# Splitting the state updates off the sample group's DeltaNet stream

## The chip, the cores and the metric

The program runs on one core of a Trainium2 chip. A core has five engines with an instruction queue each: PE (TensorE, matrix products into the accumulators of PSUM), DVE (VectorE), ACT (ScalarE), POOL (GpSimd) and SP, which here only issues DMA transfers. A queue is served in order. The metric is device time in microseconds (us); lower is better.

## The reference, cut to what matters

One decoder layer is run for a prompt of 512 tokens and for a sample group of 8 sequences with 4 new tokens each; both share the weights, so the kernel carries their 544 columns together. The layer is a half-step SwiGLU, then a token mixer, then another half-step SwiGLU, each between RMS norms:

```python
proj = h @ p['w_in']                               # one projection, D_IN = 7696
o_dn, S_new = gated_delta_rule(q, k, v, g, beta, S0)    # branch A; S0 (8 seq, 8 heads, 128, 128)
o_dn = rmsnorm(o_dn, dn_norm) * silu(z)
o_sw = attend(q_sw, k_sw, v_sw, sinks)             # branch B, window 128
y = sigmoid(gate_a) * o_dn + sigmoid(gate_b) * o_sw
x = x + g2 * rmsnorm(y @ w_out, mix_norm_post)
```

For the sample group the delta rule starts from a stored state S0 per sequence and head. It gives two results: the outputs o (from q, the old state and the four new tokens), which go on into y, and the new state S = exp(g) S0 + k^T v, which goes only to the output `delta_sample`. The two share the corrected values v, and neither needs the other after that.

## The kernel before, in words

Activations lie transposed (channels on partitions, 544 tokens along the free axis, as two halves of 272). Every weight product is made from three products of split operands (`mm3`, L301: hi by xh, hi by xl, lo by xh). A unit of weights is a 256 KB load (`raw`, L279, 4 buffers), a cast on ACT (L270, `hi`) and a subtraction on DVE or POOL (L271, `lo`); two units make one output block of 128 channels (`pb`).

The order of the work is made by `Streams`: a main generator (the weight products) and side generators each yield `(cost, latency)`. `now` grows by the cost, and a side generator is due again at `now + 1.5 * latency`; all that are due are stepped before main goes on. Of several that are due, the one with the lower rank goes first. One unit of cost stands for about a microsecond of PE: 24 matmuls of `mm3` cost 2.8 units. The framework takes the order in which instructions were emitted as their priority and builds each engine's queue from that with a cost model of its own, so that an instruction emitted late can stand earlier in its engine's queue than ones emitted before it, if its inputs are there.

In the mixer main projects, in this order, heads (U0 to U3), keys, values, queries and the gates G0 to G7. Gate block b gives `gbs` (L1521), then `z` (L1528, L1534) and the sample's part of it, `zs` (L1535). Beside it run `delta_stream` (the prompt's DeltaNet, two heads at a time, whose last norm makes `ro0` and `prb`, L340 to L345 and L353), `merge_stream` (the prompt's merge into `osw`, L1555 and L1557) and `att_main`: the attention and, after it, `delta_sample(hg)` for head groups 0 and 1, one after the other, from one set of buffers (`sdn`, one copy of each tile, four of S0).

`delta_sample` goes through these steps: decays and products of keys (to L1624), the products with the old states (`pks`, L1638), the corrected values `svn` (L1647), the outputs and `stq`, the sum under the norm (L1659). Then it updates the states: `vm` on DVE (L1662), four scalings of S0 on POOL (L1667), eight products `psu` on PE (L1673), eight additions on DVE (L1677), four stores of 512 KB from SP (L1680). Only then comes the norm of the outputs: `pro` (L1682), `srx` (L1684), eleven small DVE instructions of `rsqrt` (`sroy`, `sroa`, L340 to L345), `prb` (L353), `so` (L1689), and the merge into `osw` (L1700, L1703, L1704), which needs `zs` of the group's four heads. `merged[8]` and `merged[9]` say that the two groups are merged.

After the gates main makes `y @ w_out`. The first two output blocks (b = 0, 1) take one unit of each first: rows 0 to 511, blocks 0 to 3 of `osw` (split into `hh` and `hl` by L270 and L271); this needs `merged[8]`. Then it waits for `merged[9]`, splits blocks 4 to 7, and emits the rest only when every side stream has ended:

```python
for b in range(4, 8):
    while not (mx.merged[b] and mx.merged[9]):
        yield 0.5
    L.split(hh[:, b, :], hl[:, b, :], mx.osw[:, b, :])
while sch.side:
    yield 0.5
mx.c_sp.close()
mx.ctx.close()
```

With that the mixer's pools are closed and new ones opened in their room. In these lie `xT` (2.2 MB, reloaded, L1940) and the twelve units of `w_out` for blocks 2 to 7, which are kept (`fhw`, `flw`) since the two halves of tokens are done one after the other. The first cast into `fhw` waits until all uses of the closed pools have ended, the stores from S0 among them. Each unit of such a block is 12 matmuls.

Of the kernel before, what the change touches and what calls it, by code (L numbers as in the profile page):

```python
# [10 lines left out]
F32 = mybir.dt.float32  # L11
# [3 lines left out]
ALU = mybir.AluOpType  # L15
# [4 lines left out]
P = 128  # L20
# [14 lines left out]
EPS = 1e-6  # L35
# [24 lines left out]
L_SMP = 0.8  # L60
# [727 lines left out]
class Mixer:  # L788
# [770 lines left out]
    def delta_sample(self, hg, sp):  # L1559

        nc, L, a = self.nc, self.L, self.a
        st = L.st
        hs = slice(4 * hg, 4 * hg + 4)
        col = slice(32 + hg, 33 + hg)
        k4 = self.kqs[:, hs, 0, :]
# [6 lines left out]
        E4 = grow.rearrange("p (h s t) -> p h s t", h=4, s=SB)  # L1572
# [13 lines left out]
        kdec = sp.tile([P, P], F32, tag="skdec", name="skdec")  # L1586
# [31 lines left out]
        tq = sp.tile([P, P], F32, tag="stq", name="stq")  # L1618
        nc.scalar.activation(out=tq, in_=qcf, func=AF.Square, scale=math.sqrt(EPS * 128.0))
        S0 = []  # L1620
# [6 lines left out]
        for i, src in enumerate((kc, qc)):  # L1627
            km = sp.tile([P, 4, SB, NS], F32, tag="km", name="km")
            nc.gpsimd.memset(km, 0.0)
            for h in range(4):  # L1630
# [3 lines left out]
                                        op=ALU.mult)  # L1634
            yield 0.0, 3.0 * L_SMP
            for s in range(SB):
                for h in range(4):
                    nc.tensor.matmul(out=pk[32 * h:32 * h + 32, i * P:(i + 1) * P], lhsT=km[:, h, s, :],  # L1638
                                     rhs=S0[h][:, s, :], start=s == 0, stop=s == SB - 1, skip_group_check=True)
# [6 lines left out]
        vn = sp.tile([P, P], F32, tag="svn", name="svn")  # L1646
# [8 lines left out]
        o = sp.tile([P, P], F32, tag="so4", name="so4")  # L1655
# [2 lines left out]
        nc.scalar.activation(out=o2, in_=oT, func=AF.Square, scale=128.0 ** -0.5)  # L1658
        nc.vector.tensor_tensor(out=tq, in0=tq, in1=o2, op=ALU.add)  # L1659
        yield 0.5, 0.6 * L_SMP  # L1660
        vm = sp.tile([P, SB, P], F32, tag="km", name="vm")
        nc.vector.tensor_tensor(out=vm, in0=vn.unsqueeze(1).to_broadcast([P, SB, P]),  # L1662
                                in1=L.c("SEQM").unsqueeze(2).to_broadcast([P, SB, P]), op=ALU.mult)
        for h0 in (0, 2):
            hs = (h0, h0 + 1)
            for h in hs:
                nc.gpsimd.tensor_tensor(out=S0[h], in0=S0[h], in1=E4[:, h, :, ST - 1:ST].to_broadcast([P, SB, P]),  # L1667
                                        op=ALU.mult)
            yield 0.0, 3.0 * L_SMP
            for s0 in (0, 4):  # L1670
                p3s = [L.wk("psu4") for _ in hs]
                for h, p3 in zip(hs, p3s):
                    nc.tensor.matmul(out=p3, lhsT=kdec[32 * h:32 * h + 32, :], rhs=vm[32 * h:32 * h + 32, s0:s0 + 4, :],  # L1673
                                     start=True, stop=True)
# [3 lines left out]
                yield 1.0, 0.5 * L_SMP  # L1678
            for h in hs:
                nc.sync.dma_start(out=a["delta_sample"][0, :, 4 * hg + h].rearrange("s k v -> k s v"), in_=S0[h])  # L1680
        pr = L.wk("pro4")
        nc.tensor.matmul(out=pr[:, :64], lhsT=tq, rhs=L.ones[:, :64], start=True, stop=True)  # L1682
        rx = st.tile([P, 1], F32, tag="srx", name="srx")
        nc.vector.tensor_scalar(out=rx, in0=pr[:, 0:1], scalar1=128.0 * EPS * EPS, scalar2=None, op0=ALU.add)  # L1684
        ro = L.rsqrt(rx, [P, 1], "sro")
        yield 0.3, 3.5 * L_SMP
        pb = L.wk("prb4")
        L.bcast_cols(ro, [(0, 0, P)], [pb[:, :P]], "sro")
        nc.vector.tensor_tensor(out=o, in0=o, in1=pb[:, :P], op=ALU.mult)  # L1689
        yield 0.3, 0.3 * L_SMP  # L1690
        while any(self.z[h] is None or not self.gb_done[h] for h in range(4 * hg, 4 * hg + 4)):
            yield 0.0, 1.0 * L_SMP
        self.merge_sample(hg, o)
        self.merged[8 + hg] = True

    def merge_sample(self, hg, o):
        nc, L = self.nc, self.L
# [68 lines left out]
    def plan(self, feed):  # L1766

        L, win, x = self.L, self.win, self.x
        self.att_done = [0] * 4
        self.kqv, self.z, self.gb_done = {}, [None] * NH, [False] * NH  # L1770
        self.od_done, self.merged = [False] * NH, [False] * 10
        self.decays_done = False
        self.odd = L.dr.tile([NH, P, SEQ], F32, name="odd")
        qT, kT = (lambda: self.qT), (lambda: self.kT)
        q = lambda c: [u for b in range(8) for u in L.project(win, Q0 + b * P, x, self.evac(qT, b, (c,)), cs=(c,),
                                                              pool_lo=False)]
        self.mark0 = feed.add(q(0))
        self.marks = []

        def ba(ps):  # L1780
            self.sch.spawn(self.decays(ps, self.rp), 0)

        for n in ORDER:
            if n == "B":
                us = L.project(win, BA0, x, ba, ncol=16)
            elif n == "Q":
                us = q(1)
            elif n == "K":
                us = [u for b in range(2) for u in L.project(win, K0 + b * P, x, self.evac(kT, b))]
            elif n == "V":  # L1790
                us = [u for b in range(2) for u in L.project(win, V0 + b * P, x, self.v_block(b))]
            elif n[0] == "U":
                us = self.head_blocks(int(n[1]))
            else:
                us = self.gate_blocks(int(n[1]))
            self.marks.append((n, feed.add(us)))
# [186 lines left out]
```

## Time and profile before

| | us |
|---|---|
| three runs, median (lowest, highest) | 1589.41 (1588.27, 1590.55) |
| the profiled execution, its own time | 1595.09 |
| its span in the trace | 1593.3 |

| engine | busy us | share of the span |
|---|---|---|
| PE | 1519.0 | 95% |
| DVE | 851.2 | 53% |
| ACT | 633.5 | 40% |
| POOL | 284.3 | 18% |

The busy share is an average over stages. PE is busy nearly throughout, so the stretches in which it isn't, and those in which its granted clock is below 1.00, are what can be given back without taking work away. A time in the trace counts from the start of the span. In a timeline, "x4" is a run of four instructions of one kind merged into a piece, and the bracket gives the idle time before it and what ended that. The matrix instructions of f32 operands (`psu`, `pks`, `pro`, `prb`) show as two matmuls each.

### The profile page before, as it was taken

The page shows a single profiled execution, that of the slowest core. Times are in us where ns is not written, and L with a number is a line of the kernel's source. Part 1 is how long each engine was busy: PE and PEld are TensorE (multiplying, and loading weights), DVE is VectorE, ACT ScalarE, POOL GpSimd, SP SyncE. Part 2 cuts the span into 40 slices and gives each one's busy share as a digit, 9 for nine tenths or more (in the row PEclk, how much of TensorE's full clock was granted, in tenths as well). Part 3 has the DMA queues.
Part 4 walks back from the last instruction along what each step waited for, and adds up shares of the span by engine and source line. Part 5 has one row for each costly group of instructions (what it writes and reads, how often), then busy time and mean ns, then how long its engine had stood idle before and what let it go on. Part 6 is the DMA issues. An engine that isn't in the chain of part 4 may idle for free.

```text
span 1593.3 us, 32457 instructions
## 1 busy us (share of the span) xinstructions
PE 1519.0 (95%) x12819; PEld 1410.3 (89%) x12819; DVE 851.2 (53%) x2080; ACT 633.5 (40%) x1397; POOL 284.3 (18%) x386
## 2 busy tenths in 40 slices
PE   7999999999998999998999999998979999999996
PEld 3699999999987999897788899897979999999995
DVE  5433322333588787468879757748374332233365
ACT  4322222322444554344676433233455332223363
POOL 1000000000353232123012012312548000000042
PEclk9999999999999999899999999998989999999999
DMA  9464444455556434554212325534425433333253
GB/s 316 152 197 134 142 151 146 151 159 152 180 157 188 118 90 101 137 146 96 57 37 73 91 71 140 154 84 137 132 65 159 109 86 88 92 88 92 80 149 117
DMA packets 314533, 199.64 MB, mean 125 GB/s; under 512 B 36464, under 2 KB 297331, under 8 KB 314092
## 3 DMA queue, kind: packets, MB, share of 16 engines
q1 hardware_dynamic: 314086, 197.46, 43.6%
q8 instruction: 100, 1.64, 0.4%
q14 instruction: 53, 0.43, 0.1%
q10 hardware_dynamic: 294, 0.11, 0.0%
HBM read 182.08 MB, written 16.36 MB: 125 GB/s over the span
## 4 chain that ended last, share of the span: by engine, by line
PE 79%; DVE 12%; ACT 4%; DMA 3%; issue 2%; POOL 1%; SPq 0%; DVEq 0%; ACTq 0%; POOLq 0%
PE pb L301 17%; PE pg L301 16%; PE pu L301 16%; PE pd L301 15%; PE adaps L467 3%; DVE y L1195 2%; DVE lo L271 1%; PE psc L1010 1%; ACT hi L270 1%; PE pov L1066 1%; PE pgu L301 1%; DVE xT L571 1%; PE pvn L1332 1%; PE ppt L1052 1%; ACT s L1031 1%
## 5 line engine op out<-in xcount | busy, mean ns | idle before, releaser
L270 ACT CAST hi<-raw 128x512 fp32r<-128x512 f32 (+2 forms) x502 | 287.8, 581 | 600.5 <-PE pu L301 172.7
L271 DVE TENSOR_TENSOR lo<-raw,hi 128x512 fp32r<-128x512 f32 (+2 forms) x368 | 252.9, 688 | 397.6 <-ACT hi L270 387.4
L301 PE MATMUL pb<-hh,hi 128*128 128x272 f32 (+1 forms) x1008 | 235.7, 304 | 4.6 <-ACT hh L270 1.8
L301 PE MATMUL pb<-hl,hi 128*128 128x272 f32 (+1 forms) x1008 | 227.6, 295 | 0.0
L301 PE MATMUL pb<-hh,lo 128*128 128x272 f32 (+1 forms) x1008 | 225.9, 295 | 0.3 <-DVE lo L271 0.2
L271 POOL TENSOR_TENSOR lo<-raw,hi 128x512 fp32r<-128x512 f32 (+1 forms) x104 | 136.4, 1316 | 478.5 <-ACT hi L270 461.0
L301 PEld LDWEIGHTS pb<-hh,hi 128*128 128x128 f32 (+1 forms) x1008 | 165.7, 192 | 16.2 <-issue 8.0
L301 PE MATMUL pd<-fh,hi 128*128 128x272 f32 x704 | 171.4, 290 | 0.0
L301 PE MATMUL pd<-fl,hi 128*128 128x272 f32 x704 | 170.3, 289 | 0.0
L301 PEld LDWEIGHTS pb<-hl,hi 128*128 128x128 f32 (+1 forms) x1008 | 165.9, 191 | 2.5 <-issue 1.5
L301 PEld LDWEIGHTS pb<-hh,lo 128*128 128x128 f32 (+1 forms) x1008 | 164.7, 191 | 3.3 <-DVE lo L271 1.3
L301 PE MATMUL pd<-fh,lo 128*128 128x272 f32 x672 | 162.5, 289 | 3.5 <-DVE lo L271 1.9
L301 PE MATMUL pg<-hh,hi 128*128 128x272 f32 x672 | 150.4, 294 | 7.4 <-ACT hh L538 3.6
L301 PE MATMUL pu<-hh,hi 128*128 128x272 f32 x672 | 149.0, 292 | 0.0
L301 PE MATMUL pg<-hl,hi 128*128 128x272 f32 x672 | 147.4, 290 | 0.2 <-DVE hl L539 0.2
L301 PE MATMUL pu<-hl,hi 128*128 128x272 f32 x672 | 146.4, 289 | 0.0
L301 PE MATMUL pu<-hh,lo 128*128 128x272 f32 x672 | 145.8, 289 | 0.7 <-POOL lo L271 0.7
L301 PE MATMUL pg<-hh,lo 128*128 128x272 f32 x672 | 145.7, 288 | 0.0
L301 PEld LDWEIGHTS pd<-fh,hi 128*128 128x128 f32 x704 | 120.0, 188 | 8.6 <-issue 4.2
L301 PEld LDWEIGHTS pg<-hh,hi 128*128 128x128 f32 x672 | 109.2, 190 | 20.3 <-ACT hh L538 5.6
L301 PEld LDWEIGHTS pd<-fl,hi 128*128 128x128 f32 x704 | 120.3, 188 | 0.0
L301 PEld LDWEIGHTS pd<-fh,lo 128*128 128x128 f32 x672 | 114.1, 188 | 5.2 <-DVE lo L271 3.0
(445 smaller groups left out, 2506.4 us busy)
## 6 DMA issues: line engine op xcount, KB each, us to landing
raw<-w_in SPq DMA_DIRECT2D x136, 256.0 KB
wa<-w_ada SPq DMA_DIRECT2D x56, 512.0 KB
raw<-ffn_w_gate SPq DMA_DIRECT2D x94, 256.0 KB
raw<-ffn_w_up SPq DMA_DIRECT2D x94, 256.0 KB
raw<-ffn_w_down SPq DMA_DIRECT2D x92, 256.0 KB
wb<-w_ada SPq DMA_DIRECT2D x32, 256.0 KB
S<-state_delta SPq DMA_DIRECT2D x8, 512.0 KB
delta_sample<-S SPq DMA_DIRECT2D x8, 512.0 KB
```

What stands on the lines that cost most here:

```text
L270: self.nc.scalar.copy(out=hi, in_=raw)
L271: (eng or self.nc.vector).tensor_tensor(out=lo, in0=raw, in1=hi.bitcast(F32), op=ALU.subtract)
L301: self.nc.tensor.matmul(out=ps[:m, c, :TH], lhsT=a[:r, kt, :m], rhs=b[:r, kx, c * TH:(c + 1) * TH], start=first and i == 0, stop=last and ...
L467: self.ada_mm = nc.tensor.matmul(out=ps[32 * j:32 * j + 32, :], lhsT=self.cT[:, k, :], rhs=was[j], start=k == 0, stop=k == 7, skip_group_c ...
L571: nc.vector.tensor_tensor(out=self.xT[:, b, s], in0=self.xT[:, b, s], in1=t[:, :n], op=ALU.add)
L1010: nc.tensor.matmul(out=pss[h][:, i * 256:i * 256 + nk], lhsT=self.qT[64 * h:64 * h + 64, 2 * g + i, qb * P:(qb + 1) * P], rhs=self.kd[64 * ...
L1031: nc.scalar.activation(out=ss[h][:, i, :nk], in_=ss[h][:, i, :nk], func=AF.Exp, bias=nm[:, h, i:i + 1], accum_out=den[:, h, i:i + 1])
L1052: nc.tensor.transpose(out=ps[:, (2 * h + i) * P:(2 * h + i + 1) * P], in_=ss[h][:, i, kb * P:(kb + 1) * P], identity=L.ident)
L1066: nc.tensor.matmul(out=po[64 * h:64 * h + 64, :256], lhsT=self.vn[:, c, 64 * g:64 * g + 64], rhs=pTs[kb][:, 2 * h:2 * h + 2, :], start=kb ...
L1195: nc.vector.scalar_tensor_tensor(out=y[:, :CVN], in0=cv[:, i:i + CVN], scalar=w[i], in1=y[:, :CVN], op0=ALU.mult, op1=ALU.add)
L1332: nc.tensor.matmul(out=p2[:, n * P:(n + 1) * P], lhsT=X[:, ms[n], :], rhs=R[:, n, :] if c else vs[:, ms[n], :], start=True, stop=True)
```

## The change

`delta_sample` is cut in two. When `stq` is there it spawns a side stream `update_states` of rank 1, which does the former update with its instructions unchanged, and itself goes on at once with the norm and the merge. `updating` is true from the spawn to the end of the update, and the next `delta_sample` waits at its top while it is, since both use the same buffers. No instruction is added or taken away; the update begins with one yield of latency 0.5.

```diff
 def delta_sample(self, hg, sp):
         st = L.st
+        while self.updating:
+            yield 0.0, 1.0
         hs = slice(4 * hg, 4 * hg + 4)
...
         nc.vector.tensor_tensor(out=tq, in0=tq, in1=o2, op=ALU.add)
         yield 0.5, 0.6 * L_SMP
+        self.updating = True
+        self.sch.spawn(self.update_states(hg, sp, S0, E4, kdec, vn), 1)
+        pr = L.wk("pro4")
+        nc.tensor.matmul(out=pr[:, :64], lhsT=tq, rhs=L.ones[:, :64], start=True, stop=True)
...
+        ro = L.rsqrt(rx, [P, 1], "sro")
+        yield 0.3, 3.5 * L_SMP
...
+        self.merge_sample(hg, o)
+        self.merged[8 + hg] = True
+
+    def update_states(self, hg, sp, S0, E4, kdec, vn):
+
+        nc, L, a = self.nc, self.L, self.a
+        yield 0.0, 0.5
         vm = sp.tile([P, SB, P], F32, tag="km", name="vm")
...
             for h in hs:
                 nc.sync.dma_start(out=a["delta_sample"][0, :, 4 * hg + h].rearrange("s k v -> k s v"), in_=S0[h])
-        pr = L.wk("pro4")
-        nc.tensor.matmul(out=pr[:, :64], lhsT=tq, rhs=L.ones[:, :64], start=True, stop=True)
...
-        self.merge_sample(hg, o)
-        self.merged[8 + hg] = True
+        self.updating = False
```

Within the update the yields are: 3.0 x 0.8 of latency after each pair of scalings, and a cost of 1.0 with 0.5 x 0.8 of latency after each pair of products and additions. The norm yields a cost of 0.3 with 3.5 x 0.8 of latency, then 0.3 with 0.3 x 0.8.

## Rows read from the trace of the kernel before

**Rows 1.** The page: busy time of PE, and the chain that ended last by engine.
```profile
PE 1519.0 (95%) x12819; PEld 1410.3 (89%) x12819; DVE 851.2 (53%) x2080; ACT 633.5 (40%) x1397; POOL 284.3 (18%) x386
...
PE 79%; DVE 12%; ACT 4%; DMA 3%; issue 2%; POOL 1%; SPq 0%; DVEq 0%; ACTq 0%; POOLq 0%
```
**Rows 2.** Stretches: length, busy us of PE, PEld, DVE, ACT, POOL; clock; DMA, GB/s.
```profile
1030.00:1040.00 10.00, 10.00 (x140) 9.03 (x140) 6.71 (x27) 2.80 (x6) 1.48 (x2) 1.00 0.96 262
...
1080.00:1085.00 5.00, 2.78 (x24) 2.56 (x23) 4.32 (x7) 0.27 (x1) 5.00 (x4) 1.00 0.02 9
1085.00:1090.00 5.00, 5.00 (x42) 5.00 (x42) 5.00 (x7) 4.41 (x9) 1.23 (x1) 1.00 0.63 198
...
1102.00:1108.60 6.60, 1.13 (x5) 0.48 (x3) 4.74 (x19) 0.67 (x2) 0.00 (x0) 0.69 0.84 240
...
1112.00:1114.00 2.00, 2.00 (x10) 2.00 (x10) 2.00 (x2) 0.61 (x2) 0.92 (x1) 0.50 0.95 278
...
1116.00:1120.00 4.00, 4.00 (x34) 4.00 (x33) 0.69 (x1) 3.54 (x8) 1.52 (x2) 1.00 0.87 322
```
**Rows 3.** The chain that ended last, 1085 to 1109 (start, length, what).
```profile
1085.81 6.02 PE pb L301 x48
...
1102.11 1.88 DVE S L1677 x3
1103.99 0.08 DVE srx L1684
...
1106.33 0.46 PE prb L353
...
1107.60 0.30 DVE osw L1704
1107.93 0.65 ACT hh L270
...
1108.63 27.27 PE pb L301 x192
```
**Rows 4.** Timeline around the end of the mixer (start, length, engine, line, instruction).
```profile
1078.69 7.54 POOL L1667 TENSOR_TENSOR S<-S,sgrow 128x1024 f32<-128x1024 f32 x4 [1.93 <-PE pks L1638]
1078.80 1.83 DVE L344 TENSOR_TENSOR ro0a<-ro0a,ro0y 128x8 f32<-128x8 f32 x1
...
1087.83 0.28 DVE L1659 TENSOR_TENSOR stq<-stq,so 128x128 f32<-128x128 f32 x1
...
1095.05 0.21 POOL L1535 COPY zs<-z 128x32 f32<-128x32 f32 x1 [8.82 <-DVE z L1534]
...
1096.94 0.69 DVE L1557 TENSOR_TENSOR osw<-osw,odm 128x512 f32<-128x512 f32 x1
...
1100.28 1.99 PE L1673 MATMUL psu<-vm,skdec 32*128 32x512 f32 x8
```
**Rows 5.** Timelines of PE, ACT, SP and DVE: what follows the split of the outputs.
```profile
1102.25 0.44 PE L1682 MATMUL pro<-ones,stq 128*128 128x64 f32 x2
...
1117.48 0.29 PE L301 MATMUL pb<-hh,fhw 128*128 128x272 f32 x1
...
1109.03 2.17 ACT L270 CAST fhw<-raw 128x512 fp32r<-128x512 f32 x4
...
1103.42 1.00 SPq L1680 DMA_DIRECT2D delta_sample<-S  x2
...
1125.65 1.47 DVE L271 TENSOR_TENSOR flw<-raw,fhw 128x512 fp32r<-128x512 f32 x2 [7.36 <-ACT fhw L270]
```
**Rows 6.** Stretches of one microsecond, with Rows 2's columns: the DMA share falls.
```profile
1107.00:1108.00 1.00, 0.00 (x0) 0.00 (x0) 0.75 (x3) 0.07 (x1) 0.00 (x0) 0.50 0.94 284
1108.00:1109.00 1.00, 0.37 (x1) 0.38 (x2) 0.39 (x1) 1.00 (x2) 0.00 (x0) 0.50 0.03 8
```
**Rows 7.** Instructions of one line or tile (ns min/median/max, first and last start us).
```profile
L1684 DVE TENSOR_SCALAR srx<-pro x2: 152/152/152, 1030.2 to 1103.9; 128x1 f32<-128x1 f32 x2
...
L1704 DVE TENSOR_TENSOR osw<-osw,so x2: 292/292/293, 1038.0 to 1107.6; 128x128 f32<-128x128 f32 x2
```

More of the change, by code (lines that the diff above doesn't have):

```diff
@@ L1660, in delta_sample @@
         yield 0.5, 0.6 * L_SMP
+        self.updating = True
+        self.sch.spawn(self.update_states(hg, sp, S0, E4, kdec, vn), 1)
+        pr = L.wk("pro4")
+        nc.tensor.matmul(out=pr[:, :64], lhsT=tq, rhs=L.ones[:, :64], start=True, stop=True)
+        rx = st.tile([P, 1], F32, tag="srx", name="srx")
+        nc.vector.tensor_scalar(out=rx, in0=pr[:, 0:1], scalar1=128.0 * EPS * EPS, scalar2=None, op0=ALU.add)
+        ro = L.rsqrt(rx, [P, 1], "sro")
+        yield 0.3, 3.5 * L_SMP
+        pb = L.wk("prb4")
+        L.bcast_cols(ro, [(0, 0, P)], [pb[:, :P]], "sro")
+        nc.vector.tensor_tensor(out=o, in0=o, in1=pb[:, :P], op=ALU.mult)
+        yield 0.3, 0.3 * L_SMP
+        while any(self.z[h] is None or not self.gb_done[h] for h in range(4 * hg, 4 * hg + 4)):
+            yield 0.0, 1.0 * L_SMP
+        self.merge_sample(hg, o)
[3 more added lines that the diff above has]
+        yield 0.0, 0.5
         vm = sp.tile([P, SB, P], F32, tag="km", name="vm")
@@ L1680, in delta_sample @@
                 nc.sync.dma_start(out=a["delta_sample"][0, :, 4 * hg + h].rearrange("s k v -> k s v"), in_=S0[h])
-        pr = L.wk("pro4")
-        nc.tensor.matmul(out=pr[:, :64], lhsT=tq, rhs=L.ones[:, :64], start=True, stop=True)
[L1683 to L1692, printed above, removed]
-        self.merge_sample(hg, o)
-        self.merged[8 + hg] = True
+        self.updating = False
     def merge_sample(self, hg, o):
@@ L1771, in plan @@
         self.od_done, self.merged = [False] * NH, [False] * 10
-        self.decays_done = False
+        self.decays_done = self.updating = False
         self.odd = L.dr.tile([NH, P, SEQ], F32, name="odd")
```

## The prediction, made before the changed kernel was run

> **What bounds the kernel now.** I read the page first: PE is busy 95% of the span, and 79% of the chain that ended last runs on it [rows 1]. So a change that takes no work away pays only where PE stands still or runs at a low clock, and I looked for such places near the code that is moved, in a table of stretches. There are two [rows 2]. From 1080 to 1085 PE is busy 2.78 of 5 us. From 1102 to 1108.6 it is busy 1.13 of 6.6; the granted clock, 1.00 before, falls to 0.50 (the lower of the two levels, 1.2 GHz) and is still 0.50 at 1112 to 1114, when PE has long been full again; by 1116 to 1120 it is back at 1.00.
>
> The chain of waits says what the second hole is [rows 3]: the four last additions to the states end at 1103.99, then come `srx`, eleven small DVE instructions, the broadcast `prb` at 1106.33, the merge into `osw` (to 1107.90), the first split of block 4, and PE starts the second halves of `w_out` at 1108.63. That is the norm of the second head group, the piece that the change takes from behind the update. Its input `stq` was there at 1088.11 [rows 4], 16 us before `srx`.
>
> **The change part by part.** It adds and removes no instruction; everything is order.
>
> 1. The norm moved ahead of the update, group 1. In the hole, PE waits from 1100.28, where the first halves of `w_out` end and the last four products of the update follow, to 1108.63: 8.35 us. The products take 1.99 of it [rows 4] and must run somewhere; `pro` (starts 0.22 apart, two of them in 0.44) and `prb` (0.46) as well [rows 3, 5]; I put these at 0.45 together, since they overlap their neighbours. So 8.35 - 1.99 - 0.45 = 5.9 us of idle time can go.
>
> What is late next? The merge also needs `zs` of the last gate block, copied by 1095.26, and block 7 needs the prompt's merge, done at 1097.63 [rows 4]. From `prb` to the end of the merge the old kernel took 1.11 us (1106.79 to 1107.90), then one cast of 0.65 and one subtraction a block [rows 3]. Block 4 is split by about 1097, block 7 by about 1100, and PE wants it only from 1102.3 on, once the products are through. The norm itself, from 1088.1, has 7 us for a run that took 2.4 from `srx` to `prb` [rows 3]; DVE is full there (5.00 of 5 us from 1085 to 1090 [rows 2]), but what fills it is partly the update, which no longer stands ahead.
>
> 2. The clock. After the hole the 48 matmuls of the first kind ran from 1108.63 to 1117.48, 8.85 us [rows 3, 5]; 48 like them took 6.02 us at the full clock [rows 3]. If PE doesn't stand still, the clock has no cause to fall: 2.83 us come back. The 2.22 us of idle time at 1080 left the clock at 1.00 [rows 2], so a small rest of the hole would not undo this. Together 5.9 + 2.8 = 8.7 us.
>
> 3. The kept weights. This is the cap on the gain. The first cast into `fhw` needs the closed pools free, the last stores from S0 included. They are issued at 1103.42 to 1104.42 [rows 5], the DMA engines are busy 0.94 of the microsecond to 1108 and 0.03 of the next [rows 6], so they land at 1108.0; the casts start at 1109.03 and PE uses the first kept unit at 1117.48 [rows 5], 8.45 us later. That looks like slack, but the ninth unit has less: its subtraction runs from 1125.65, 0.7 us long, since its load waited for buffers of the earlier ones and for the 2.2 MB of `xT`; PE wants it at 1117.48 + 8 x 1.51 = 1129.6 (12 matmuls at 6.02/48 us). Slack 3.3 us. So the gain is the smaller of 8.7 and 3.3 plus what the casts move forward.
>
> They move with the update's end. In the old stream the norm of group 0 stood between the first update and the start of group 1; by its yields that is 0.3 + 1.5 x 2.8 + 0.3 + 1.5 x 0.24 = 5.2 units, on the trace 8.1 us (`srx` 1030.2 to the end of the last merge instruction 1038.3 [rows 7]). Now group 1 starts when the update ends, later by its first yield (0.75) and up to 1.5 for the poll: 3.0 to 4.4 units earlier than before, and a unit is about 3.0/2.8 us (24 matmuls): 3.2 to 4.7 us. By the trace's 8.1 it could be 7; by no head start, zero. I take 4.0, near the yields, since they write the order. The gain is then 3.3 + 4.0 = 7.3, with 3.3 and 8.7 as its ends.
>
> 4. Group 0. Its norm delays nothing but group 1's start; PE has work from the gates all the while. Nothing, or down to a microsecond either way.
>
> 5. The hole at 1080 to 1085. PE waits there for `ro0`, the norm of the prompt's last two heads. An instruction of that chain with 8 elements took 1.83 us while POOL scaled S0 (four in 7.54 us, 1.89 each) [rows 4]; its like in the hole after took 0.2. With group 1 some 4 us earlier the scaling would begin at about 1074.7 and lie over the whole of `ro0`, 1077 on: up to 1.4 us more of waiting, or all 2.2 gone if it has passed. I take nothing. The Trainium skill, SBUF — State Buffer, section "Who interferes with whom", says that a DVE instruction with two SBUF inputs and a GpSimd one that reads SBUF lock each other out for a whole instruction; the trace agrees (1.83 against 0.2 us), and by that rule alone the sum would be 7.3 - 1.4 = 5.9, because the change frees POOL's scaling to slide over a norm.
>
> 6. The new wait at the top of `delta_sample`, and the queues. It is a wait in the order of emission, not an instruction; what it holds back is group 1, which waited for more before. Stores from S0 stand in SP's queue ahead of weight loads as before, only some 4 us earlier; `xT` is free when block 7 is split, so it may go ahead of the loads for blocks 4 to 7. 2.2 MB at the 322 GB/s of [rows 2] is 7 us; I count it as inside the 3.3 us of slack, since these transfers stood in the same row before. Uncovered, it would cost 1 to 2 us.
>
> Sum: 7.3 us. The profiled execution took 1595.09 us (span 1593.3, 1.8 around it) and would take 1587.8. The median of the runs is 1589.41, 5.7 below the profiled one; the same gain there gives **1582.1**.
>
> **The rivals.** A: the kept weights don't move. If the last stores land at 1108 as before, only 3.3 us are gained: 1586.1. For it: the update ends last in the old order, and the norm now competes with it on a full DVE. Against it: group 1 waits for less.
>
> B: the stall changes place. `pro` and `prb` now stand in PE's queue among the gates, with DVE's small instructions between; if too few matmuls lie between, PE stands and waits, as it did 2.2 us at 1080 [rows 2]. Up to 3.6 us of the 7.3 would be lost, leaving 3.7: 1585.7. Against it: while group 0's norm ran (1030 to 1038 [rows 7]) PE was busy 10.00 of 10 us [rows 2].
>
> C, on the other side: the update falls behind. It has rank 1, and its `vm` and additions can queue on DVE after norm, merge and splits. Each microsecond by which the last stores land after 1108.0 moves the kept casts; beyond 3.3 us late there is no gain, beyond 6.5 a measurable loss. If the update began only after the merge (1096 instead of 1085, 11 us late), the loss would be 11 - 3.3 = 7.7, and 2.8 more if PE stands until its clock falls: 1597 to 1600. For it: DVE is full there, and every instruction of the norm is now ahead. Against it: the scalings on POOL start when the last product with S0 is done, 9 us before `stq`, whatever the rank [rows 4]; and main emits nothing more until the update has ended.
>
> D: nothing moves. The queues are built by the framework's own model, which may have put the merge and splits where they are for another reason: within 3 us of 1589.4.
>
> **How the numbers follow.** My forecast 0.55, with its own range 1579 to 1586 (from 8.7 gained plus up to 2 us from the hole at 1080, to rival A's edge); A 0.17, B 0.10, C 0.12, D 0.06. A measurement of this kernel can tell about 0.2%, 3.2 us, from no change: the line is at 1586.2. A lies on it and counts half to each side, as does B; so faster 0.55 + 0.09 + 0.05 = 0.69, the same 0.08 + 0.05 + 0.06 = 0.19, slower 0.12. The range of eight in ten is 1577.5 to 1590.5: below, the first three terms with the hole at 1080 gone and a late surprise; above, D and the mild end of C.
>
> **What would show it.** Right: `srx` of group 1 soon after `stq`, ahead of the last additions; `hh` of block 4 cast by about 1098; no gap of PE over 2 us after the first halves of `w_out`, and a clock of 1.00 through the following 20 us; the last stores issued near 1100 and the kept casts near 1104. Step 3 is wrong if PE waits in the kept units for `flw`, or if the casts start no earlier and PE doesn't wait. Step 5 shows in the idle time before `prb` of the prompt. The whole is wrong if the hole of 6 us is still there, or if an equal one stands elsewhere between 1010 and 1130.

## The result: slower, and the profile after

The changed kernel took 1598.4 us (median of four runs, 1596.07 to 1601.57) against 1588.84 (1586.51 to 1590.55) of the kernel before on the same chip: a ratio of 1.0053, interval 1.0027 to 1.0079. The forecast was 1582.1, faster. The profiled execution took 1596.07 us, span 1594.3; that of before had 1595.09. These two lie only 1 us apart because the one of before lost time long before the change: every engine's queue is the same up to group 0's norm, and yet it is 8.2 us later there (3.6 of them arose from 660 to 680, where PE was busy 18.19 of 20 us at a clock of 0.74; the kernel after had 1.00 there). So both are counted from one instruction in front of the change, the load of group 0's decays, before and after:

```profile
L1567 SPq DMA_DIRECT2D sgrow<-gcd x1: 320/320/320, 966.0 to 966.0; - x1
```
```profile
L1569 SPq DMA_DIRECT2D sgrow<-gcd x1: 320/320/320, 957.8 to 957.8; - x1
```

From there to the first kept unit (`pb` from `fhw`) before takes 151.5 us (to 1117.48 [rows 5]) and after 159.0 (to 1116.80): 7.5 us lost, and 1.6 more to the end. The page's line of the chain answers the second of [rows 1]: less of it is PE, more DMA.

```profile
PE 76%; DVE 12%; DMA 4%; ACT 4%; issue 2%; POOL 1%; SPq 0%; ACTq 0%; DVEq 0%; POOLq 0%
```

The stretches of after, with the columns of [rows 2]:

```profile
1075.00:1080.00 5.00, 0.52 (x3) 0.55 (x3) 4.83 (x11) 0.36 (x1) 3.70 (x2) 0.90 0.02 8
1080.00:1085.00 5.00, 5.00 (x23) 5.00 (x23) 2.24 (x17) 0.00 (x0) 0.00 (x0) 0.50 0.15 45
...
1102.00:1104.00 2.00, 2.00 (x16) 1.58 (x13) 1.49 (x3) 0.37 (x1) 0.70 (x1) 1.00 0.40 118
...
1112.00:1116.00 4.00, 0.00 (x0) 0.00 (x0) 1.29 (x3) 1.94 (x4) 0.00 (x0) 1.00 0.98 409
1116.00:1120.00 4.00, 3.20 (x14) 3.20 (x15) 0.61 (x2) 2.55 (x7) 2.87 (x3) 0.57 0.97 317
```

The old hole is gone: PE is full from 1102 to 1104. Two others are there. One is at 1075 to 1080, with the clock at 0.50 for the 5 us behind it, the other at 1112 to 1117. The table of waits (PE's idle time from 950 to 1130: in total, times, longest) names them:

```profile
PE pb L301 <- ACT dacc L1899: 4.8, 1, 4.8
PE pro L1666 <- DVE ro0a L344: 4.5, 1, 4.5
PE pro L1666 <- DVE stq L1661: 2.0, 1, 2.0
```

The third row is group 0's `pro` at 1001.63. The second is put down to `ro0a`, the last instruction that ended before PE went on; but the operand of `pro` is `stq`, which had ended 0.15 us before `pro` started. The timeline of that hole, DVE, POOL and PE:

```profile
1067.86 6.11 POOL L1690 TENSOR_TENSOR S<-S,sgrow 128x1024 f32<-128x1024 f32 x3 [0.44 <-PE pks L1640]
...
1070.03 2.16 DVE L271 TENSOR_TENSOR lo<-raw,hi 128x512 fp32r<-128x512 f32 x1
1072.12 2.40 DVE L1519 SCALAR_TENSOR_TENSOR osw<-tg,osw 128x512 f32<-128x512 f32 x1
1074.44 1.23 DVE L1685 TENSOR_TENSOR vm<-svn,cst 128x1024 f32<-128x1024 f32 x1
1074.55 2.89 POOL L1690 TENSOR_TENSOR S<-S,sgrow 128x1024 f32<-128x1024 f32 x1
...
1075.66 1.92 DVE L1713 SCALAR_TENSOR_TENSOR osw<-gbs,osw 128x128 f32<-128x128 f32 x1
1077.50 1.22 DVE L340 TENSOR_SCALAR ro0y<-rx 128x8 int32<-128x8 int32 x1
...
1079.05 0.28 DVE L1661 TENSOR_TENSOR stq<-stq,so 128x128 f32<-128x128 f32 x1
...
1079.48 0.66 PE L1666 MATMUL pro<-ones,stq 128*128 128x64 f32 x2 [4.53 <-DVE ro0a L344]
...
1085.49 1.19 PE L353 MATMUL prb<-ident,ro0y 128*128 128x128 f32 x8
```

DVE is busy throughout, but while POOL scales S0 three of its instructions (`lo`, and `osw` twice) take three to seven times as long as without the scaling (experiment 2); `ro0y` takes 1.22 us beside a subtraction on POOL (`lo`, 1077.39 to 1078.69). PE has 12 matmuls between the group's outputs and `pro`, and stands from 1074.95. The prompt's `prb` is queued behind `pro` and 24 matmuls, 22 of which take 5.11 us at the low clock, and so comes at 1085.49. The chain of after (start, length, what) runs from there straight to the second hole:

```profile
1080.14 5.11 PE pb L301 x22
...
1086.66 0.61 DVE od L1377
...
1087.28 4.64 DMA odd<-od
...
1091.94 2.70 DMA odm<-odd
...
1097.72 4.76 DMA odm<-odd
...
1102.51 0.75 DVE odm L1555
...
1106.33 1.20 DVE S L1700 x2
...
1107.55 6.42 DMA delta_sample<-S
...
1114.59 1.65 ACT fhw L270 x3
1116.24 0.52 ACT dacc L1899
...
1116.80 7.74 PE pb L301 x48
```

The prompt's outputs go through memory (`odd`, `odm`). The merge that reads them (L1555) stands in DVE's queue ahead of the last four additions to the states, and two splits (`hl`) stand between these; behind those come the last stores; these must land before ACT's casts of the kept weights start; and `dacc`, which PE needs to go on, stands behind four of the casts. The 48 matmuls then take 7.74 us (6.02 at the full clock [rows 3]).

In us from the load of the decays, with three kernels of the experiments (starts, but for the addition):

| | before | after | no scaling | delay | delay, ACT scales |
|---|---|---|---|---|---|
| `stq`, group 1 | 121.8 | 121.3 | 114.6 | 118.7 | 115.8 |
| `pro`, group 1 | 136.2 | 121.7 | 115.4 | 125.3 | 125.9 |
| `prb` of the prompt | 116.5 | 127.7 | 118.6 | 120.5 | 121.1 |
| last addition to S0 ends | 138.0 | 149.7 | 140.3 | 141.0 | 139.4 |
| first kept cast | 143.0 | 156.3 | 146.5 | 145.7 | 143.2 |
| first kept unit on PE | 151.5 | 159.0 | 149.3 | 148.5 | 146.0 |

`stq` was as late before (121.8 against 121.3). There it cost nothing, since PE asked for it 14 us later. The change made PE ask for it at once. The last three columns are experiments 2, 4 and 10.

### The profile page after: what moved, and what is told of

It is laid out like the page before. It is cut to its first block, busy times and chain, and to the rows that moved or that the text cites. A ratio compares the mean times of both kernels' runs of the same rounds, so it can differ in the third digit from the quotient of the medians.

```text
span 1594.3 us, 32447 instructions
## 1 busy us (share of the span) xinstructions
PE 1514.2 (95%) x12819; PEld 1406.0 (88%) x12819; DVE 852.8 (53%) x2080; ACT 634.6 (40%) x1397; POOL 287.2 (18%) x386
## 4 chain that ended last, share of the span: by engine, by line
PE 76%; DVE 12%; DMA 4%; ACT 4%; issue 2%; POOL 1%; SPq 0%; ACTq 0%; DVEq 0%; POOLq 0%
PE pg L301 16%; PE pu L301 16%; PE pb L301 15%; PE pd L301 15%; PE adaps L467 3%; DVE y L1195 2%; DVE lo L271 2%; PE psc L1010 1%; ACT hi L270 1%; PE pov L1066 1%; PE pgu L301 1%; DVE xT L571 1%; PE ppt L1052 1%; ACT s L1031 1%; PE pvn L1332 1%
## 5 line engine op out<-in xcount | busy, mean ns | idle before, releaser
L301 PE MATMUL pu<-hh,lo 128*128 128x272 f32 x672 | 145.7, 288 | 0.7 <-POOL lo L271 0.7
```

The lines of the kernel that those rows point to most:

```text
L301: self.nc.tensor.matmul(out=ps[:m, c, :TH], lhsT=a[:r, kt, :m], rhs=b[:r, kx, c * TH:(c + 1) * TH], start=first and i == 0, stop=last and ...
```

## The experiments

All were timed in five rounds beside the kernel before on the same chip. Theory: `pro` stands in PE's in-order queue ahead of work that is ready, `stq` is late because POOL's scaling slows DVE (the two lock each other out for whole instructions), and what is behind `pro` carries the delay on to the kept weights. Rivals: the kept weights' wait for the stores is the loss by itself; or one of the two groups alone makes it.

**1. The kept weights free of the stores.** S0 gets a pool of its own, whose room isn't reused.

```diff
+            self.s0p = L.pool("s0p", 1, side="right")
-            S = sp.tile([P, SB, P], F32, tag="S0", name="S0", bufs=4)
+            S = self.s0p.tile([P, SB, P], F32, tag="S0", name="S0", bufs=4)
```

> The changed kernel, with the four S0 tiles in a pool of their own that stays open to the end, so that the room of the kept w_out weights no longer waits for the stores from S0. Theory 1 (the second hole of the changed kernel, 4.8 us of PE at 1112 to 1117 with 1.7 us at the lower clock behind it, is the wait of the kept casts for the last stores): that hole goes, the casts start with or soon after the split of block 7, and the time falls by about 6 us against the changed kernel, to a ratio of about 1.001 to 1.002 to the kernel before. Rival (the casts are late because ACT reaches them late, or PE waits for something else there): the hole stays, the ratio stays at about 1.005.

Measured: 1596.5 us, ratio 1.0053 (1.0030 to 1.0076). Nothing was gained, though the first kept cast came 7.6 us earlier than in the kernel after (148.7 in the table's measure). The wait for `dacc` is gone, and PE's waits are now:

```profile
PE pro L1666 <- DVE ro0a L344: 4.5, 1, 4.5
PE pb L301 <- DVE hl L271: 4.1, 2, 3.5
PE pro L1666 <- DVE stq L1661: 2.9, 1, 2.9
```

The waits for `pro` stay, and the second hole has only another name: DVE's subtractions for the kept weights now stand ahead of the last split `hl`, which PE needs first. So taking that wait away alone does not give the loss back.

**2. No scaling.** As after, but S0 isn't multiplied by exp(g) (the new states lack that factor). PE's queue has the same order as after.

```diff
-            for h in hs:
-                nc.gpsimd.tensor_tensor(out=S0[h], in0=S0[h], in1=E4[:, h, :, ST - 1:ST].to_broadcast([P, SB, P]),
-                                        op=ALU.mult)
```

> The changed kernel without the scaling of S0 by exp(g) in the update (this leaves out eight POOL instructions of 1.9 us, so the new states miss that factor). Theory 2 (the first hole, 4.5 us of PE before pro with 2.9 us at the lower clock behind it, comes from DVE instructions that are locked out while POOL scales S0): DVE's instructions ahead of stq take 0.3 to 0.7 us each instead of 1.2 to 2.4, the wait before pro falls below 1.5 us, the clock stays at 1.00, and the time falls by 6 to 7 us against the changed kernel, to a ratio of about 1.001. Rival (PE waits because pro simply stands too early in its queue, whatever DVE's instructions take): a wait of 3 us or more stays, ratio 1.004 or more.

Measured: 1588.65 us, ratio 0.9998 (0.9983 to 1.0012): the loss is gone. The same DVE instructions, in the same place:

```profile
1070.23 0.68 DVE L271 TENSOR_TENSOR lo<-raw,hi 128x512 fp32r<-128x512 f32 x1
1070.84 0.69 DVE L1519 SCALAR_TENSOR_TENSOR osw<-tg,osw 128x512 f32<-128x512 f32 x1
1071.45 1.21 DVE L1685 TENSOR_TENSOR vm<-svn,cst 128x1024 f32<-128x1024 f32 x1
...
1073.28 0.28 DVE L1710 SCALAR_TENSOR_TENSOR osw<-gbs,osw 128x128 f32<-128x128 f32 x1
1073.48 0.16 DVE L340 TENSOR_SCALAR ro0y<-rx 128x8 int32<-128x8 int32 x1
...
1074.17 0.29 DVE L1661 TENSOR_TENSOR stq<-stq,so 128x128 f32<-128x128 f32 x1
...
1075.00 0.33 PE L1666 MATMUL pro<-ones,stq 128*128 128x64 f32 x2
```

The four that are quicker give back 1.5, 1.7, 1.6 and 1.1 us, together 5.9; the last 1.1 is `ro0y`, free since POOL's subtraction now comes behind `stq`. `stq` comes 6.7 us earlier by the table, `pro` of group 1 doesn't wait, and the clock stays at 1.00 there. A wait of 4.5 us for `dacc` is still there: even so the last additions stand behind the prompt's merge, and their stores take 6.08 us to land. So the second hole needs no first one. Without the first it only comes 10 us earlier, and the first kept unit at 149.3 instead of 159.0.

**3. No scaling in the kernel before.** The same edit there, to see whether the scaling costs something whatever the order.

> The kernel before without the scaling of S0 by exp(g) on POOL (this leaves out eight POOL instructions, so the new states miss that factor); PE's queue is in the same order as in the kernel before. Theory 2 (the lock between POOL's scaling and DVE hits the changed kernel's order far more than the old one): only the wait of 2.2 us before the prompt's prb goes, ratio 0.998 to 0.9995, so that without the scaling the change is worth about zero instead of costing 8 us. Rival (the lock costs both orders the same): ratio 0.994 to 0.996, and the change costs 8 us without it as well.

Measured: 1587.03 us, ratio 1.0000 (0.9984 to 1.0015). PE's wait of 2.2 us before the prompt's `prb` is gone from the trace, but within this interval, some 2.4 us either way, the scaling cost nothing in the old order.

**4. The norm's first matmul later.** The scaling stays on POOL, and POOL's and SP's queues are those of after; one yield makes `pro` due nine units of cost later.

```diff
+        yield 0.0, 6.0
         pr = L.wk("pro4")
```

> The changed kernel with one yield of latency 6 (9 units) ahead of the norm's first product pro, so that PE has other matmuls ahead of it; the scaling stays on POOL. If PE's loss at the first hole comes from standing behind pro in its queue: the wait before pro falls below 1 us, and the ratio falls to 1.000 to 1.002. Rival (DVE is late whatever stands in PE's queue): the wait goes to the prompt's prb or to the split of block 4, ratio 1.004 or more.

Measured: 1585.63 us, ratio 0.9991 (0.9978 to 1.0003), against 1.0053 without that line. PE's waits:

```profile
PE prb L353 <- DVE sroy L345: 2.2, 1, 2.2
PE prb L353 <- DVE ro0y L345: 1.4, 1, 1.4
PE pb L301 <- ACT dacc L1900: 1.1, 1, 1.1
```

No wait for `pro` is left, the prompt's `prb` passes it in the queue (120.5 and 125.3 in the table), and the second hole shrinks from 4.8 to 1.1 us; its `xT` is issued 1.5 us behind the last stores instead of 0.3, and these land after 4.66 us. With experiment 2 this shows the cause in the changed kernel from both sides: either the lock goes or `pro` stands later, and the loss goes.

**5, 6. One group only.** Group 1 alone as in the change (the other's update inline), then group 0 alone.

```diff
-        self.sch.spawn(self.update_states(hg, sp, S0, E4, kdec, vn), 1)
+        if hg == 1:          # 6: hg == 0
+            self.sch.spawn(self.update_states(hg, sp, S0, E4, kdec, vn), 1)
+        else:
+            yield from self.update_states(hg, sp, S0, E4, kdec, vn)
```

> Only the second head group is cut in two; the first does update, norm and merge in one stream as in the kernel before, so that the second group starts at its old time. If the loss lies in what the second group's own split does (pro early in PE's queue, additions of the update behind the prompt's merge, late stores): about as the changed kernel, ratio 1.004 to 1.006. Rival (the loss comes from the second group's earlier start, which slides POOL's scaling over the norm of the prompt's last heads): faster than the kernel before, ratio 0.995 to 0.998.

> Only the first head group is cut in two; the second does update, norm and merge in one stream as in the kernel before, but may start 3 to 4 us earlier. If the loss lies in the second group's own split: as the kernel before, 0.998 to 1.001, with the old hole before the second halves of w_out. Rival (the loss comes from the second group's earlier start): the wait before pro or prb near 1080 is there, ratio 1.002 to 1.005.

Measured: group 1 alone 1594.24 us, ratio 1.0044 (1.0030 to 1.0058); group 0 alone 1597.49, ratio 1.0051 (1.0032 to 1.0070). Each half costs about as much as both. Waits with group 1 alone, then with group 0 alone:

```profile
PE pb L301 <- ACT dacc L1902: 8.6, 1, 8.6
```
```profile
PE pb L301 <- ACT hh L270: 4.7, 1, 4.7
PE prb L353 <- DVE sroy L345: 2.7, 1, 2.7
PE pro L1669 <- DVE stq L1661: 2.4, 1, 2.4
```

With group 1 alone there is no wait for `pro`, and the largest wait by far is at the kept weights. The norm's `prb` stands in PE's queue ahead of the update's products, which start 7.3 us later from the load of the decays than before (133.1 against 125.7), though `stq` is as early (122.2 against 121.8). The last stores are issued 4.6 us later, behind `xT` (1096.30), and land after 10.15 us:

```profile
1089.66 0.32 PE prb L353
1089.98 1.92 PE psu L1699 x8
```

With group 0 alone the early `pro` is group 0's, followed by a low clock (0.53 from 1000 to 1002, 0.62 to 1004), and the old hole comes back larger (7.4 us, where it was 3.6 + 1.8 before). The trace shows why it is larger: the merge of group 1 ended at 1101.86, but ACT's queue has four kept casts ahead of the split of block 4, and they wait until the last stores have landed:

```profile
1102.71 2.18 ACT fhw L270 x4
1104.88 0.56 ACT hh L270
```

This misses the first expectation of experiment 6 (0.998 to 1.001). So the groups don't add up, and the early `pro` is not the only way to the loss: where the kept casts hold up ACT's queue, or PE, until the last stores have landed, it comes as well.

**7, 8. The scaling on another engine, S0 apart.** On DVE, then on ACT (32 activations of 128 columns a group).

```diff
-                nc.gpsimd.tensor_tensor(out=S0[h], ...)
+                nc.vector.tensor_tensor(out=S0[h], ...)                 # 7
+                for s in range(SB):                                     # 8
+                    nc.scalar.activation(out=S0[h][:, s, :], in_=S0[h][:, s, :], func=AF.Copy,
+                                         scale=E4[:, h, s, ST - 1:ST])
```

> The changed kernel with the scaling of S0 on DVE (four instructions a group, some 1.1 us each without the lock) and S0 in a pool that stays open. Theory 1 and 2 together: no DVE instruction ahead of stq above 1.3 us, both holes below 2 us, ratio 0.995 to 0.998. Rival (4.4 us more of DVE a group, in order ahead of stq and of the splits, take the place of the lock): PE waits for stq or hl, ratio 1.000 or more.

> The changed kernel with the scaling of S0 on ACT (32 instructions of 128x128 a group, some 0.3 us each, instead of 4 on POOL) and S0 in a pool that stays open. Theory 1 and 2 together (the two holes come from the lock and from the kept weights' wait for the stores): both holes go, ratio 0.994 to 0.997. Rival (ACT's 10 us of scaling in order ahead of its casts of weights takes the place of the lock): PE waits for hi or hh on ACT, ratio 0.999 or more.

Measured: 1590.1 us, ratio 1.0003 (0.9989 to 1.0018), and 1587.9, ratio 1.0000 (0.9983 to 1.0017). Off POOL the waits for `pro` shrink to 0.2 and 0.9 us and the loss goes, as without any scaling; but `hl` keeps PE waiting 4.5 and 4.6 us, as in experiment 1, and the gain that both theories expected (0.994 to 0.998) doesn't come.

**9, 10, 11. More on top of the delay.** With S0 apart as in 1 (9); with the scaling on ACT as in 8, S0 not apart (10); with a longer delay (11):

```diff
-        yield 0.0, 6.0
+        yield 0.0, 12.0                                               # 11
```

> The kernel after with the six units of delay ahead of the norm's first matmul, and S0 in a pool of its own, so that the kept weights' casts wait for no store. Theory: with the delay (1585.6 us) what is left in front of the kept units is a wait of 1.1 us and about 5 us from the issue of the last stores to their landing; if the casts need not wait for that, they come 3 to 5 us earlier, the wait of 1.1 us goes, and nothing else changes: 1583 to 1585. Rival: the place of the kept casts' last instructions in DVE's queue decides, as in the kernel with S0 apart and no delay: the subtractions for the kept weights come out ahead of the splits of the merged blocks and hold them up, a wait on hl of 3 to 4 us stands in PE's queue, and the time is 1586 to 1590.

> The kernel after with the delay, and the scaling of S0 done by ACT in 32 small activations a group instead of by POOL; S0 stays in its pool. Theory: POOL's scaling still slows DVE in the kernel with the delay (an osw merge of 1.93 us, ro0y 1.19, and waits of PE for prb of 2.2 and 1.4 us). Without the lock the waits for prb shrink to about 1 us in all, 2 to 3 us less: 1582.5 to 1584. Rival: the delay already hides the lock, and 64 activations stand ahead of ACT's casts: no gain or a loss, 1585 to 1589.

> The kernel after with twelve units of delay instead of six. If PE standing early behind the norm's first matmul is the whole cause and six units already clear it, twelve change nothing there (the wait for pro is 0 in both) and only push prb and the merge later in PE's queue: 1585 to 1587. If the rest of the waits (prb of the second group, 2.2 us) is of the same kind, they go too: 1583 to 1584. Rival: the norm's later end pushes the splits of the merged blocks towards the second halves of w_out, the old hole comes back by 2 to 4 us: 1588 to 1590.

Measured: 1586.57 us, ratio 0.9983 (0.9968 to 0.9999); **1582.32, ratio 0.9971 (0.9959 to 0.9983)**; 1586.36, ratio 0.9991 (0.9977 to 1.0005). The first and the third can't be told from the delay alone. The second beats the kernel before and the kernel after; from the delay alone (0.9978 to 1.0003) its interval is not quite apart. ACT's scaling without the delay was run only with S0 apart (8). What PE still waits for there at the second group's norm and the kept weights:

```profile
PE prb L353 <- DVE sroy L345: 0.7, 1, 0.7
PE pb L301 <- ACT dacc L1901: 0.6, 1, 0.6
```

The longer delay brings the old hole back in part (`prb` from `sroy` 2.1 us, `hh` 1.8): a longer delay isn't better.

**12. The scaling on ACT in the kernel before** (the edit of 8, S0 not apart), to see whether that gain is ACT's alone.

> The kernel before with the scaling of S0 done by ACT in 32 small activations a group instead of by POOL, its order otherwise untouched. Theory: the gain of the fastest kernel (order, delay and ACT's scaling, ratio 0.9971) needs the order, because without any scaling the kernel before took as long as with it (ratio 1.0000); here too the hole of 6 us before the second halves of w_out stays: ratio 0.999 to 1.002, 1586 to 1591 us. Rival: that gain is ACT's scaling alone, which lets DVE end the prompt's norm sooner, and the order adds nothing: ratio about 0.997, 1582 to 1584 us.

Measured: 1589.09 us, ratio 0.9993 (0.9977 to 1.0009). By the medians it isn't, though the ends of the two intervals overlap. The trace shows the old hole untouched:

```profile
PE prb L353 <- DVE sroy L345: 3.6, 1, 3.6
PE pb L301 <- ACT hh L270: 1.8, 1, 1.8
```

## Why the prediction was wrong

The step that failed first is step 1, with step 2 behind it (the old hole, 8.7 us). The hole goes as described: `srx` of group 1 at 1080.33 and no gap behind the first halves of `w_out`. The step failed in its premise that the norm only has to fit into DVE's time. `pro` and `prb` are also places in PE's queue, and those were priced at 0.45 us, as work. As waits the two groups' `pro` cost 4.5 and 2.0 us, and the clock fell after all, some 20 us ahead of where the step looked, counted from the load of the decays: 22 matmuls behind the first hole took 5.11 us, 2.4 more than at 6.02/48 us each [rows 3].

Step 5 (the hole at 1080) is where the lock was seen and mis-sized. It was priced on the eight-element instructions of `ro0`, at most 1.4 us, and then put at nothing. What counted is what stands ahead of `stq`, 5.9 us by experiment 2: 4.8 in three big DVE instructions beside the scaling, and 1.1 in `ro0y` beside POOL's subtraction. The sentence that cited the Trainium skill (SBUF — State Buffer, "Who interferes with whom") held: two-input instructions took 2.16 against 0.68 us and 1.92 against 0.28, and the block goes both ways, POOL's scaling taking 2.89 us where `vm` had started 0.11 earlier, and 2.04 on average in the run of three. The same section of the Trainium skill counts `tensor_scalar` among the operations that can contend by a two-port mode, when their operands meet its conditions; the trace fits that, as `ro0y` from one input took 1.22 us beside a subtraction on POOL, and 0.16 without, but no row shows the mode itself. The rule was applied to the wrong victims.

Step 3 (the kept weights) has the right mechanism and the wrong sign. The scaling of group 1 did begin earlier, by 2.6 us from the common mark (4.0 forecast). But the last addition ended 11.8 us later and the first kept cast started 13.3 us later, instead of 4.0 earlier. The slack of 3.3 us, which was worked out for the ninth unit, was used up, and PE waited 4.8 at the first.

Step 4 (group 0 costs nothing) failed: with group 0 alone in the new order the kernel is 0.51% slower. The row that stood against rival B, PE busy 10.00 of 10 us while the old norm of group 0 ran [rows 2], showed that norm behind its update, not right behind the outputs.

Step 6 was right to fear `xT`. It is issued 0.26 us behind the last of the store issues, and those stores took 6.42 us, where before the DMA share fell 4.0 us after the last issue (1104.02 to 1108.0 [rows 6]): some 2.4 us, a little over the 1 to 2 named there, but put down as covered.

Of the rivals, B (PE stands behind `pro`) had the mechanism, at a price of at most 3.6 us for what cost 6.5 and the clock. C had the time (1597 to 1600) and the price (each microsecond by which the stores land late), but in the changed kernel that is luck: the products of group 1 start 4.7 us later than before (130.4 against 125.7), which PE's stand at `pro` and the low clock behind it (4.5 + 2.4) cover, and the last additions were held behind the prompt's merge, which B's stall had delayed. With group 1 alone, where nothing waits for `pro`, the update does fall behind the norm as C said. B and C were kept apart as two cases when one can delay the other. A and D are out.

Part of the forecast gain exists, with two more changes: with the norm's matmul later and the scaling off POOL the kernel is 0.29% faster, 4.6 us of the 7.3, and its first kept unit comes 5.5 us earlier than before by the table. Open is how the loss splits between the first hole and the second. The first delays what the second waits for, but the second is there without it (experiment 2), and either half alone loses about as much as both.

## What to carry to other kernels

Before an instruction is moved forward in the program, read how late its operand really is at the new place: an operand that was late for nobody (`stq`) becomes a stall of the whole in-order queue once its reader stands early. A lock between two engines that costs nothing measurable in one order (ratio 1.0000 without it) can be needed for the whole of a loss in another (1.0053 with it, 0.9998 without), so it is priced on everything that stands ahead of the first reader, not on the instruction where it was noticed. And follow what is queued behind the stalled instruction to its end: here PE stood 4.5 us at `pro`, the prompt's `prb` behind it came 11 us later than before, and the kept casts 13.

## What the runs showed of the hardware that was not expected

The landing time of the same stores went with what was issued next to them: 3.74 us in the fastest kernel and 4.66 with the delay, where `xT` (2.2 MB) was issued 1.5 us behind the last of them, 6.08 (no scaling) and 6.42 (after) where it followed after 0.3 us, 10.15 (group 1 alone) where it stood ahead. That `xT` made the difference was not tested by itself.

A pause of PE of 2.2 us left the clock at 1.00 in the kernel before (the hole at 1080 to 1085 [rows 2]). With group 1 alone the same wait for `ro0y` was also 2.2 us, and there the clock was 0.50 from 1076 to 1078, and the 12 matmuls behind it took 2.70 us instead of 1.5. So the one row that step 2 relied on did not settle what such a pause does. And PE's clock can fall without a pause that the rows show: in the fastest kernel it was at 0.50 from 1028 to 1030, though PE was busy 2.00 of 2 us in the row ahead. What it had run there were state products, then 32 matmuls of 32 by 32 and eight of the usual kind. The clock was low from about 1027.7 to 1031.2, which cost an estimated 1.7 us, half of that stretch.

```profile
1026.00:1028.00 2.00, 2.00 (x26) 1.81 (x25) 1.19 (x6) 0.73 (x2) 0.52 (x1) 0.94 0.40 126
1028.00:1030.00 2.00, 2.00 (x11) 2.00 (x10) 0.57 (x1) 1.20 (x2) 0.00 (x0) 0.50 0.95 285
```
